# One plain chunk instead of two at the start of each feed-forward block, and a new order of products and operand sums

## The chip, the cores and the metric

The kernel runs on one core of one Trainium2 chip. The metric is the device time of one execution in microseconds (us). Smaller is better.

## The reference

The trunk has two layers. A layer is half a feed-forward block, a token mixer (HGRN2 in layer 0, windowed attention in layer 1), and half a feed-forward block again, each behind an RMSNorm; so there are four feed-forward blocks, called f0 to f3 here. The tokens of both requests (512 and 256) share the weights.

```
D_MODEL = 1024; D_FF = 2816; DEPTH = 2
def swiglu_ffn(x, w1, w2):                     # all float32
    gate, up = jnp.split(x @ w1, 2, axis=-1)   # w1: 1024 x 5632
    return (jax.nn.silu(gate) * up) @ w2       # w2: 2816 x 1024
for li in range(DEPTH):
    x = x + 0.5 * swiglu_ffn(rmsnorm(x, norm_g[li, 0]), ffn_w1[li, 0], ffn_w2[li, 0])
    x = x + mixer(rmsnorm(x, norm_g[li, 1]))   # hgrn2_mixer, then window_gqa_mixer
    x = x + 0.5 * swiglu_ffn(rmsnorm(x, norm_g[li, 2]), ffn_w1[li, 1], ffn_w2[li, 1])
return rmsnorm(x, final_norm_g)
```

## The kernel before

**Products.** A float32 product is three matmuls: each operand is split into a high part (a cast on ScalarE) and a low part (a subtraction on VectorE), and TensorE multiplies high by high, high by low, low by high into one bank of PSUM (`mm3`, L288 to L290, and `product`, L527). `split` (L293 and L294) does it for operands, L229 and L230 for weights, L186 and L189 for the weights of plain chunks.

**Seven products.** The feed-forward blocks use a Strassen-Winograd form. The 768 tokens are two halves of 384 columns, the model width is two halves of 512. The turned (transposed) token blocks are b00, b10, b01, b11, and four sums of them are t1 to t4. Product p1 multiplies a weight block with b00, p2 with b10, p3 with b11, p4 with t4, p5 with t1, p6 with t2, p7 with t3. One chunk is 128 hidden columns. A chunk by seven products (`up_pair`) is 7 x 4 x 3 = 84 matmuls of 384 columns; a plain chunk (`up_plain`, two token halves, gate and up column, eight blocks of the width) is 2 x 2 x 8 x 3 = 96. A block has 22 chunks: two plain ones (0 and 1), whose first half needs only b00 and b10, then twenty by seven products. After each group of four chunks the down products follow (`down_quad`, L608).

**Operand sums.** When the second token half has been turned and split (b01, b11), `sums` makes t1 to t4: for each of two column groups `kp` four subtractions (L441, L442, L444, L445) and four splits of 128 x 768 elements. VectorE does them while TensorE works on the plain chunks.

**Weights.** SyncE's queue (SP) loads the raw blocks: two "wr" tiles of 512 KB (gate, up) and one "s" tile of 256 KB (for p7) a chunk. There are four wr buffers and two s buffers. GpSimd (POOL) issues accumulating transfers: s += first block of wr, and in place wr += wr (L153). VectorE adds twice into wr (L243), for p6 and p3. `split` in `quad_steps` makes one "w" tile for each product (L229, L230); there are eight. `plan_ffn` queues the loads, `load_next` issues a load when raw buffers are free, and `ahead` stages the next product's weights whenever TensorE frees a w tile.

**Order.** Each engine works in its own order, which a tile scheduler derives from the program's order, the dependences and a few hints (`issue_after`). So the diff alone does not give the order on an engine. In the rows of this order "waits" names what an instruction waits for: an engine (Activation is ScalarE, Pool is GpSimd), a transfer of SP's queue (DMAHW) or one of GpSimd's (DMASW).

Of the kernel before, what the change touches and what calls it, by code (L numbers as in the profile page):

```python
# [49 lines left out]
class Trunk:  # L50
    def __init__(self, ctx, tc, consts):
# [103 lines left out]
    def load_next(self):  # L155
# [43 lines left out]
    def quad_steps(self, key, raws, srcs, order):  # L199
# [36 lines left out]
        sums = {"p6": (a11, a21), "p3": (a12, a11)}  # L236
        last = [None]

        def step(name):
            if name in sums:  # L240
                into, term = sums[name]
                with self.tc.issue_after(last[0]):
                    nc.vector.tensor_add(into, into, term)  # L243
# [292 lines left out]
    def up_pair(self, tag, j, hold=False):  # L536
        nc = self.nc
        key = (tag, j)
# [1040 lines left out]
```

## Time and profile before

| | |
|---|---|
| time, median of 3 runs | 2731.84 us (2731.38, 2731.84, 2732.61) |
| span of the profiled execution | 2730.5 us, mean granted TensorE clock 0.999 |
| TensorE (PE) busy | 2720.2 us, 100% |
| VectorE (DVE) busy | 2110.3 us, 77% |
| ScalarE (ACT) busy | 1339.0 us, 49% |
| GpSimd (POOL) busy | 204.8 us, 7% |

The span runs from the first to the last instruction of the profiled execution; for that execution no other time is given, and the three times above are those of the timed runs. The span lies 1.3 us below their median. Matmuls are pipelined, so the duration of one row (334 ns) is longer than the step from one to the next.

### The profile page before, as it was taken

Reading aid. Unit: us, or ns where it says so; the run is one execution under the profiler, and the core shown is the slowest. Engines: PE = TensorE matmul, PEld = TensorE weight load, DVE = VectorE, ACT = ScalarE, POOL = GpSimd, SP = SyncE. Lnnn points to the kernel's source line nnn. Section 1 sums busy time; section 2 is a strip of 40 time slices with the busy share of each in tenths; the row PEclk is TensorE's granted clock in tenths of the full one; section 3 lists DMA queues with packets and bytes.
Section 4 is the critical chain, followed back from the end, with each engine's and each line's share of the span. In section 5 each row is a group of like instructions: output and inputs, shape, how many; then the busy total and the mean of one; then the engine's idle time right before and its main releaser. Section 6 shows DMA issues by size and latency. Waiting matters only on the chain.

```text
span 2730.5 us, 44549 instructions
## 1 busy us (share of the span) xinstructions
PE 2720.2 (100%) x17305; PEld 2483.8 (91%) x17305; DVE 2110.3 (77%) x3789; ACT 1339.0 (49%) x2507; POOL 204.8 (7%) x243
## 2 busy tenths in 40 slices
PE   9999999999999999999999999999999999999998
PEld 9999999889888889999999999999987789999998
DVE  8888788567476778778888878887847768787877
ACT  6444444456466554444446444444546754444443
POOL 1110110000000000111110011101000000111000
PEclk9999999999999999999999999999999999999999
DMA  6544554311110524465553355544422123555443
GB/s 183 136 123 117 127 143 120 123 56 48 55 41 25 143 65 120 113 147 129 128 121 102 88 129 139 135 116 112 133 72 78 47 62 87 130 139 135 117 112 108
DMA packets 331411, 293.98 MB, mean 108 GB/s; under 512 B 11752, under 2 KB 258240, under 8 KB 331200
## 3 DMA queue, kind: packets, MB, share of 16 engines
q1 hardware_dynamic: 294352, 212.89, 26.6%
q0 software_dynamic: 32544, 64.76, 13.6%
q10 hardware_dynamic: 4304, 13.49, 1.4%
q8 instruction: 135, 2.21, 0.3%
q14 instruction: 76, 0.62, 0.1%
HBM read 216.91 MB, written 9.44 MB: 83 GB/s over the span
## 4 chain that ended last, share of the span: by engine, by line
PE 97%; DVE 1%; ACT 1%; issue 0%; DMA 0%; DVEq 0%; SPq 0%; ACTq 0%
PE ps L527 42%; PE ps L608 21%; PE ps L288 9%; PE ps L289 9%; PE ps L290 9%; PE ps L856 1%; PE ps L643 1%; PE ps L1451 1%; PE ps L1442 1%; PE ps L1004 1%; PE ps L1390 1%; PE ps L411 1%; PE ps L980 0%; PE ps L969 0%; DVE x L671 0%
## 5 line engine op out<-in xcount | busy, mean ns | idle before, releaser
L527 PE MATMUL ps<-big,w 128*128 128x384 f32 x6720 | 1169.7, 334 | 0.6 <-ACT tA L544 0.6
L527 PEld LDWEIGHTS ps<-big,w 128*128 128x128 f32 x6720 | 1165.9, 188 | 2.8 <-ACT tA L544 1.2
L229 ACT CAST w<-wr 128x512 fp32r<-128x512 f32 (+1 forms) x606 | 424.2, 710 | 721.8 <-DVE wr L243 305.4
L230 DVE TENSOR_TENSOR w<-wr,w 128x512 fp32r<-128x512 f32 (+1 forms) x606 | 480.5, 798 | 225.4 <-ACT w L229 158.5
L608 PE MATMUL ps<-w,big 128*128 128x512 f32 x2520 | 575.4, 389 | 0.0
L608 PEld LDWEIGHTS ps<-w,big 128*128 128x128 f32 x2520 | 472.8, 188 | 97.5 <-DVE x L671 0.3
L671 DVE SCALAR_TENSOR_TENSOR x<-ps,x 128x512 f32<-128x512 f32 x468 | 302.6, 681 | 4.7 <-PE ps L290 4.7
L288 PE MATMUL ps<-w,big 128*128 128x512 f32 x576 | 232.5, 404 | 0.0
L290 PE MATMUL ps<-w,big 128*128 128x512 f32 x576 | 225.5, 391 | 0.0
L289 PE MATMUL ps<-w,big 128*128 128x512 f32 x576 | 225.1, 391 | 0.0
L288 PE MATMUL ps<-big,w 128*128 128x384 f32 (+2 forms) x640 | 217.9, 342 | 0.2
L289 PE MATMUL ps<-big,w 128*128 128x384 f32 (+2 forms) x640 | 215.8, 337 | 0.4 <-DVE big L371 0.2
L290 PE MATMUL ps<-big,w 128*128 128x384 f32 (+2 forms) x640 | 215.1, 336 | 0.0
L293 ACT CAST big<-tA 128x384 fp32r<-128x384 f32 x296 | 147.8, 512 | 117.5 <-DVE tA L572 40.4
L153 POOL DMA_DIRECT2D s<-wr x122 | 106.3, 913 | 1300.1 <-DMA wr<-in_ffn_w_dram 623.6
L189 DVE TENSOR_TENSOR w<-wr,w 128x1024 fp32r<-128x1024 f32 (+1 forms) x88 | 105.9, 1209 | 82.0 <-ACT w L186 73.4
L294 DVE TENSOR_TENSOR big<-tA,big 128x384 fp32r<-128x384 f32 x296 | 159.9, 551 | 8.2 <-ACT big L293 7.8
L153 POOL DMA_DIRECT2D wr<-wr x101 | 87.6, 868 | 1009.3 <-DVE tA L1110 386.0
L186 ACT CAST w<-wr 128x1024 fp32r<-128x1024 f32 (+1 forms) x90 | 93.0, 1035 | 93.4 <-PE ps L289 66.3
L288 PEld LDWEIGHTS ps<-w,big 128*128 128x128 f32 x576 | 108.3, 188 | 25.6 <-issue 4.6
L290 PEld LDWEIGHTS ps<-w,big 128*128 128x128 f32 x576 | 108.1, 188 | 23.5 <-issue 0.4
L289 PEld LDWEIGHTS ps<-big,w 128*128 128x128 f32 x640 | 121.0, 189 | 9.4 <-DVE big L294 1.0
(191 smaller groups left out, 2891.8 us busy)
## 6 DMA issues: line engine op xcount, KB each, us to landing
wr<-in_ffn_w_dram SPq DMA_DIRECT2D x264, 512.0 KB, 3.9
s<-wr POOLq DMA_DIRECT2D x122, 256.0 KB, 5.1
s<-in_ffn_w_dram SPq DMA_DIRECT2D x120, 256.0 KB, 3.3
wr<-wr POOLq DMA_DIRECT2D x80, 256.0 KB, 4.2
wr<-in_hg_w_in_dram SPq DMA_DIRECT2D x40, 512.0 KB, 3.8
wr<-wr POOLq DMA_DIRECT2D x21, 512.0 KB, 6.0
spill<-x ACTq DMA_DIRECT2D x12, 512.0 KB, 2.9
x<-spill ACTq DMA_DIRECT2D x12, 512.0 KB, 3.3
```

The costliest lines, as they stand in the source:

```text
L153: self.nc.gpsimd.dma_start(out, src, accum_op=ALU.add)
L189: eng.tensor_sub(lo, raw[:, ks, :], hi.bitcast(F32))
L229: nc.scalar.copy(h, src)
L230: low = nc.vector.tensor_sub(l, src, h.bitcast(F32)).ins
L288: nc.tensor.matmul(out, a[0], b[0], start=first, stop=False)
L289: nc.tensor.matmul(out, a[0], b[1], start=False, stop=False)
L290: nc.tensor.matmul(out, a[1], b[0], start=False, stop=last)
L293: self.nc.scalar.copy(hi, src)
L294: return self.nc.vector.tensor_sub(lo, src, hi.bitcast(F32)).ins
L527: self.nc.tensor.matmul(ps, a[x], b[y], start=first and k == 0 and i == 0, stop=k == 3 and i == 2, skip_group_check=True,)
L608: nc.tensor.matmul(ps, a[x], w[y], start=name == chain and kp == 0 and q == 0, stop=kp == 1 and q == 2, skip_group_check=True,)
L671: return self.nc.vector.scalar_tensor_tensor(x, ps, c, x, ALU.mult, ALU.add).ins
```

## The change

In each block only chunk 0 stays plain. Chunk 1 becomes a chunk by seven products, and chunks 1 and 2 are opened early (`open_pair`): behind the plain half 0 come p1 and p2 of both, then the plain half 1, then p3, p3, p5, p7, p5, p4, p6, p7 of the two in turn, and p6 and p4 of chunk 2. The weights of their p3 are made ahead of the operand sums: four additions into raw blocks and two splits, behind the last split of b11 (`turned`). The sums are made in the order t1, t3, t4, t2, each for both column groups. Chunk 3 does its products in another order (`THIRD`). `closed` and `open` hold back the staging of further weights until a given product is done.

```diff
--- before.py
+++ after.py
-PLAIN = 2
-GROUPS = (NF - PLAIN) // 4
+GROUPS = (NF - 2) // 4
+OPEN = ("p1", "p2", "p3", "p5", "p7", "p4", "p6")
+OPEN2 = ("p1", "p2", "p3", "p5", "p7", "p6", "p4")
+THIRD = ("p1", "p4", "p2", "p7", "p5", "p6", "p3")
...
+        if how is OPEN:
+            self.loaded.append((2, steps[:2]))
+            self.opened = steps[2:]
+        elif how is OPEN2:
+            a, b = self.opened, steps[2:]
+            self.loaded.append((0, steps[:2]))
+            entries = [(2, [a[0], b[0], a[1], a[2], b[1], a[3], a[4]]), (2, b[2:])]
+            self.closed.append(entries[0])
+            self.loaded += entries
+        elif how is THIRD:
+            self.loaded += [(0, steps[:3]), (2, steps[3:])]
+            self.closed.append(self.loaded[-1])
+        else:
+            self.loaded.append((len(raws), steps))
...
-        sums = {"p6": (a11, a21), "p3": (a12, a11)}
+        sums = {"p6": [(a11, a21)], "p3": [(a12, a11)]}
+        if order in (OPEN, OPEN2):
+            sums = {"p3": sums["p6"] + sums["p3"]}
         last = [None]
 
         def step(name):
-            if name in sums:
-                into, term = sums[name]
-                with self.tc.issue_after(last[0]):
+            for into, term in sums.get(name, ()):
+                low = self.turned if order in (OPEN, OPEN2) else last[0]
+                with self.tc.issue_after(last[0]), self.tc.issue_after(low):
                     nc.vector.tensor_add(into, into, term)
             last[0] = split(name, own[name])
...
+            if self.closed and self.loaded[0] is self.closed[0]:
+                return
             if self.held + self.loaded[0][1][0][0] > WBUFS:
                 return
             self.stage_next()
+
+    def open(self):
+        if self.closed:
+            self.closed.pop(0)
...
+            self.turned = low
...
-        for kp in range(2):
-            tiles = (self.tn[(i // 2, i % 2)][:, kp] for i in range(4))
-            self.mix(*tiles, lambda name, src: self.put(name, kp, src))
+        sub = self.nc.vector.tensor_sub
+        both = lambda f: [f(kp, *tiles[kp]) for kp in range(2)]
+        both(lambda kp, b11, b12, b21, b22: (sub(b22, b12, b22), sub(b12, b11, b12), self.put("t1", kp, b12)))
+        both(lambda kp, b11, b12, b21, b22: self.put("t3", kp, b22))
+        both(lambda kp, b11, b12, b21, b22: (sub(b11, b11, b22), sub(b21, b21, b11), self.put("t4", kp, b21)))
+        both(lambda kp, b11, b12, b21, b22: self.put("t2", kp, b11))
...
-            if i < PLAIN:
+            if i == 0:
                 self.plan((tag, i, 0), gate, (NC, P))
                 self.plan((tag, i, 1), up, (NC, P))
             else:
-                self.plan_quad((tag, i), (gate, up), (NC, P), UP)
+                self.plan_quad((tag, i), (gate, up), (NC, P), {1: OPEN, 2: OPEN2, 3: THIRD}.get(i, UP))
...
             if half:
+                if not c:
+                    self.open()
                 self.done((tag, j, c))
...
+        third = j == 3
...
-        p("p7", c, True, False)
+        p("p4" if third else "p7", c, True, False)
         nc.scalar.copy(w, c)
-        free("p7")
+        free("p4" if third else "p7")
         p("p2", a, False, True)
         nc.scalar.activation(a, a, AF.Silu)
         free("p2")
+        if third:
+            p("p7", c, False, True)
+            nc.vector.tensor_sub(w, c, w)
+            free("p7")
         p("p5", d, True, False)
         nc.vector.tensor_sub(w, w, d)
         free("p5")
-        p("p4", c, False, True)
+        if not third:
+            p("p4", c, False, True)
         p("p6", b, True, True)
         nc.vector.tensor_sub(v, v, b)
         nc.vector.tensor_sub(t, c, v)
         nc.vector.tensor_mul(t, t, a)
-        free("p4", "p6")
+        free(*(("p6",) if third else ("p4", "p6")))
...
+    def open_pair(self, tag, j, hold):
+        nc = self.nc
+        banks = {}
...
+        def gate():
+            p("p1", "a", True, False)
+            nc.scalar.copy(v, banks["a"])
+            free("p1")
+            p("p2", "a", False, True)
+            nc.scalar.activation(banks["a"], banks["a"], AF.Silu)
+            free("p2")
...
+        def p3():
+            p("p3", "d", True, False)
+            nc.scalar.copy(w, banks["d"])
+            free("p3")
+
+        def p5():
+            p("p5", "d", False, True)
+            free("p5")
+
+        def p7():
+            p("p7", "c", True, False)
+            nc.vector.tensor_add(w, w, banks["c"])
+            nc.vector.tensor_sub(w, w, banks["d"])
+            free("p7")
+
+        def p4():
+            p("p4", "c", False, True)
+            free("p4")
+
+        def p6():
+            p("p6", "b", True, True)
+            nc.vector.tensor_sub(v, v, banks["b"])
+            free("p6")
+        def results():
+            t = self.tmp(H)
+            nc.vector.tensor_sub(t, banks["c"], v)
+            nc.vector.tensor_mul(t, t, banks["a"])
+            yield t
+            nc.vector.tensor_sub(w, w, v)
+            nc.vector.tensor_add(v, v, banks["d"])
...
+            pairs = {}
             if g == 0:
-                ts = {}
-                for half in range(2):
-                    for j in range(PLAIN):
-                        t = ts[2 * j + half] = self.up_plain(tag, j, half)
-                        name = f"b{j}{half}"
...
-                gather(ts, 0)
+                first = [self.up_plain(tag, 0, 0)]
+                low = put("b00", first[0], 0)
...
+                gate, p3, p5, p7, p4, p6, results = zip(*(self.open_pair(tag, j, j == 2) for j in (1, 2)))
+                gate[0]()
+                gate[1]()
+                for j in (1, 2):
+                    self.take((tag, j, "p3"))
                 self.run_later(len(self.deferred))
+                first.append(self.up_plain(tag, 0, 1))
+                for step in (p3[0], p3[1], p5[0], p7[0], p5[1], p4[0], p6[0], p7[1]):
+                    step()
+
+                def second():
+                    p6[1]()
+                    self.open()
+                    p4[1]()
+                    yield from results[1]()
+
+                pairs[1], pairs[2] = results[0](), second()
+                pairs[0] = first
             for kp in range(2):
                 ts = []
                 for j in range(2):
-                    for half, t in enumerate(self.up_pair(tag, 4 * g + 2 * kp + j, j == 0)):
+                    n = 4 * g + 2 * kp + j
+                    for half, t in enumerate(pairs.get(n) or self.up_pair(tag, n, j == 0)):
                         ts.append(t)
                         name = f"b{j}{half}"
-                        if name != "b01":
+                        if name != "b01" and (n or half):
                             put(name, t, kp)
                 gather(ts, kp)
             self.down_quad(tag, g, hid)
```

The order on the engines shows it at three places. The first is VectorE in f0 at the last split of b11. Before, the sums follow at once (rows L441 to L445; L453 is an addition that `sums` does first).

```order
L294 TENSOR_TENSOR big_74_399<-big_70_382,big_74_399 128x2x384 [waits Activation_49]
L294 TENSOR_TENSOR big_75_402<-big_70_382,big_75_402 128x2x384 [waits Activation_49]
L453 TENSOR_TENSOR big_39_220<-big_36_204 128x768
L453 TENSOR_TENSOR big_39_220<-big_37_211 128x768
L441 TENSOR_TENSOR big_70_382<-big_63_343,big_70_382 128x768 [waits DVE_49] x2
L442 TENSOR_TENSOR big_63_343<-big_34_198,big_63_343 128x768 [waits DVE_49] x2
L444 TENSOR_TENSOR big_34_198<-big_34_198,big_70_382 128x768 [waits DVE_49]
L294 TENSOR_TENSOR big_77_422<-big_63_343,big_77_422 128x2x384 [waits Activation_49]
L445 TENSOR_TENSOR big_39_220<-big_39_220,big_34_198 128x768 [waits DVE_49]
```

After, big_76 and big_77 are b11's split; the four additions into the raw blocks of chunk 1 (wr_23, wr_24) and chunk 2 (wr_43, wr_44) and the two splits of p3's weights (w_79, w_80) come next, and then the sums.

```order
L318 TENSOR_TENSOR big_77_408<-big_72_388,big_77_408 128x2x384 [waits Activation_49]
L261 TENSOR_TENSOR wr_23_157<-wr_23_157,wr_24_159 128x512 [waits DMAHW5_49,DMASW2_49,DMASW1_49]
L261 TENSOR_TENSOR wr_43_231<-wr_43_231,wr_44_233 128x512 [waits DMASW6_49,DMASW5_49,DMAHW0_49,DVE_49,Pool_49]
L261 TENSOR_TENSOR wr_23_157<-wr_23_157 128x512 [waits DVE_49]
L261 TENSOR_TENSOR wr_43_231<-wr_43_231 128x512 [waits DVE_49]
L478 TENSOR_TENSOR big_40_224<-big_38_215 128x768
L246 TENSOR_TENSOR w_79_440<-wr_23_157,w_79_440 128x512 [waits PE_49,Activation_49]
L246 TENSOR_TENSOR w_80_445<-wr_43_231,w_80_445 128x512 [waits PE_49,Activation_49]
L483 TENSOR_TENSOR big_72_388<-big_65_348,big_72_388 128x768 x2
L483 TENSOR_TENSOR big_65_348<-big_35_202,big_65_348 128x768 [waits DVE_49] x2
L485 TENSOR_TENSOR big_35_202<-big_35_202,big_72_388 128x768 [waits DVE_49]
L318 TENSOR_TENSOR big_81_452<-big_65_348,big_81_452 128x2x384 [waits Activation_49]
```

The p3 weights moved ahead of every sum. The second addition waits for two transfers of GpSimd's queue (DMASW5, DMASW6). Behind these rows stand three splits, two sums and then the split of w_90, the weights of chunk 1's p5.

The second place is TensorE in f0, where the product p5 of chunk 1 starts. Before, the plain chunks run until the first seven-product chunk starts with p1 (ps_106), p7 (ps_108) behind it.

```order
L527 MATMUL ps_106_621<-big_32_186,w_88_495 128x384 [waits Activation_49]
L527 MATMUL ps_106_621<-big_32_186,w_88_495 128x384
L527 MATMUL ps_106_621<-big_32_186,w_88_495 128x384 [waits DVE_49]
L527 MATMUL ps_106_621<-big_32_186,w_88_495 128x384 x3
L527 MATMUL ps_106_621<-big_33_193,w_88_495 128x384 x6
L527 MATMUL ps_108_623<-big_79_430,w_89_498 128x384 [waits PE_49,Activation_49]
L527 MATMUL ps_108_623<-big_79_430,w_89_498 128x384
L527 MATMUL ps_108_623<-big_79_430,w_89_498 128x384 [waits DVE_49]
L527 MATMUL ps_108_623<-big_79_430,w_89_498 128x384 x3
```

After, ps_103 ends p3 of chunk 2, ps_106 is p7 of chunk 1 (weights w_91), ps_101 with w_90 is p5 of chunk 1 and ps_103 with w_92 p5 of chunk 2.

```order
L558 MATMUL ps_103_578<-big_76_405,w_80_445 128x384 x3
L558 MATMUL ps_103_578<-big_77_408,w_80_445 128x384 x6
L558 MATMUL ps_106_610<-big_83_460,w_91_510 128x384 [waits PE_49,Activation_49]
L558 MATMUL ps_101_561<-big_81_452,w_90_507 128x384 [waits Activation_49]
L558 MATMUL ps_101_561<-big_81_452,w_90_507 128x384 [waits DVE_49]
L558 MATMUL ps_106_610<-big_83_460,w_91_510 128x384 [waits DVE_49]
L558 MATMUL ps_103_578<-big_81_452,w_92_513 128x384 [waits Activation_49]
L558 MATMUL ps_103_578<-big_81_452,w_92_513 128x384
L558 MATMUL ps_101_561<-big_81_452,w_90_507 128x384 [waits DVE_49]
L558 MATMUL ps_101_561<-big_81_452,w_90_507 128x384 x3
L558 MATMUL ps_101_561<-big_82_457,w_90_507 128x384 x6
L558 MATMUL ps_106_610<-big_83_460,w_91_510 128x384 [waits DVE_49]
```

Six matmuls of three products stand ahead of the rest of p5 of chunk 1, which waits for VectorE.

The third place is VectorE in f1, around the last products of the two opened chunks. Before, chunk 2 (ps_1266 is its p5) has the engine to itself with splits of its own raw blocks (wr_1202, wr_1203).

```order
L294 TENSOR_TENSOR big_1261_10385<-tA_1257_10369,big_1261_10385 128x384 [waits Activation_49]
L294 TENSOR_TENSOR big_1262_10388<-tA_1230_10146,big_1262_10388 128x384 [waits Activation_49]
L230 TENSOR_TENSOR w_1272_10443<-wr_1203_10002,w_1272_10443 128x512 [waits DMASW0_49,DMAHW3_49,PE_49,Activation_49]
L556 TENSOR_TENSOR tA_1268_10396<-tA_1268_10396,ps_1266_10394 128x384 [waits PE_49]
L230 TENSOR_TENSOR w_1273_10459<-wr_1203_10002,w_1273_10459 128x512 [waits Activation_49]
L243 TENSOR_TENSOR wr_1202_10000<-wr_1202_10000,wr_1203_10002 128x512
L230 TENSOR_TENSOR w_1274_10490<-wr_1202_10000,w_1274_10490 128x512 [waits Activation_49]
```

After, ps_1272 holds p7 of chunk 2, and L652 reads it before p4 of chunk 2 adds into the same bank; w_1267, w_1269, w_1270 and w_1281 are the weights of chunk 3's p1, p4, p2 and p7, from wr_1258, wr_1259 and s3_1260.

```order
L246 TENSOR_TENSOR w_1267_10395<-wr_1258_10335,w_1267_10395 128x512 [waits DMAHW4_49,Activation_49]
L246 TENSOR_TENSOR w_1269_10413<-wr_1259_10337,w_1269_10413 128x512 [waits DMAHW5_49,Activation_49]
L246 TENSOR_TENSOR w_1270_10428<-wr_1258_10335,w_1270_10428 128x512 [waits Activation_49]
L246 TENSOR_TENSOR w_1281_10527<-s3_1260_10339,w_1281_10527 128x512 [waits DMAHW3_49,DMASW3_49,Activation_49]
L662 TENSOR_TENSOR tA_1235_10170<-tA_1235_10170,ps_1271_10443 128x384 [waits PE_49]
L667 TENSOR_TENSOR tA_1273_10472<-ps_1268_10398,tA_1235_10170 128x384 [waits DVE_49]
L670 TENSOR_TENSOR tA_1236_10171<-tA_1236_10171,tA_1235_10170 128x384
L668 TENSOR_TENSOR tA_1273_10472<-tA_1273_10472,ps_1239_10174 128x384 [waits DVE_49]
L652 TENSOR_TENSOR tA_1238_10173<-tA_1238_10173,ps_1272_10457 128x384 [waits PE_49]
```

The split of p7's weights of chunk 3 (w_1281), which waits for a transfer of SP (DMAHW3) and one of GpSimd (DMASW3), now stands ahead of L652 of chunk 2. On TensorE the matmul that adds p4 of chunk 2 into ps_1272 waits for that L652.

```order
L558 MATMUL ps_1272_10457<-big_1246_10251,w_1261_10343 128x384 x6
L558 MATMUL ps_1280_10501<-big_1249_10264,w_1264_10363 128x384 x6
L558 MATMUL ps_1280_10501<-big_1250_10267,w_1264_10363 128x384 x6
L558 MATMUL ps_1272_10457<-big_1247_10256,w_1266_10380 128x384 [waits DVE_49,Activation_49]
L558 MATMUL ps_1272_10457<-big_1247_10256,w_1266_10380 128x384 x5
L558 MATMUL ps_1272_10457<-big_1248_10261,w_1266_10380 128x384 x6
L558 MATMUL ps_1292_10563<-big_1201_9995,w_1267_10395 128x384 [waits Activation_49]
```

More of the change, by code (lines that the diff above doesn't have):

```diff
@@ L170, in load_next @@
             steps = self.quad_steps(key, raws, srcs, how)
-        self.loaded.append((len(raws), steps))
+        if how is OPEN:
[12 more added lines that the diff above has]
+            self.loaded.append((len(raws), steps))
     def wtile(self):
@@ L454, in sums @@
         self.whole = []
-        for kp in range(2):
-            tiles = (self.tn[(i // 2, i % 2)][:, kp] for i in range(4))
-            self.mix(*tiles, lambda name, src: self.put(name, kp, src))
+        tiles = [[self.tn[(i // 2, i % 2)][:, kp] for i in range(4)] for kp in range(2)]
+        sub = self.nc.vector.tensor_sub
[4 more added lines that the diff above has]
+        both(lambda kp, b11, b12, b21, b22: self.put("t2", kp, b11))
     xn = [None] * NBLK
     normed = mixed = first = halved = None
-    normal = None
+    normal = opened = turned = None
     plains = 0
@@ L509, in up_plain @@
                     self.first = None
-                if half == 0 and k in (((), (2, 6)), ((3, 7), (3, 7)))[j][c]:
+                if half == 0 and c and k in (2, 6):
                     self.run_later()
             if half:
+                if not c:
+                    self.open()
                 self.done((tag, j, c))
@@ L579, in up_pair, with p, free, finish @@
         yield w
+    def open_pair(self, tag, j, hold):
+        nc = self.nc
+        banks = {}
+        v, w = (self.tmp(H) for _ in range(2))
+        def p(name, bank, first, last):
+            if first:
+                banks[bank] = self.ps(H)
+            self.product((tag, j), name, FACTOR[name], banks[bank], first, last)
+        def free(name):
+            self.done((tag, j, name))
+        def gate():
+            p("p1", "a", True, False)
+            nc.scalar.copy(v, banks["a"])
+            free("p1")
+            self.run_later(len(self.deferred) > 1)
+            p("p2", "a", False, True)
+            nc.scalar.activation(banks["a"], banks["a"], AF.Silu)
+            free("p2")
+            self.run_later(len(self.deferred) > 1)
+        def p3():
[24 more added lines that the diff above has]
+            nc.vector.tensor_add(v, v, banks["d"])
+            def finish(after=None):
+                with self.tc.issue_after(after) if after else nullcontext():
+                    self.last_act = nc.scalar.activation(v, v, AF.Silu).ins
+                self.last_dve = nc.vector.tensor_mul(w, v, w).ins
+            if hold:
+                self.tail = finish
+            else:
+                finish()
+            yield w
+        return gate, p3, p5, p7, p4, p6, results
     def down_quad(self, tag, g, hid):
@@ L683, in gather @@
                 self.mix(ts[0], ts[1], ts[2], ts[3], lambda name, src: put(name, src, kp))
+            pairs = {}
             if g == 0:
-                ts = {}
-                for half in range(2):
-                    for j in range(PLAIN):
-                        t = ts[2 * j + half] = self.up_plain(tag, j, half)
-                        name = f"b{j}{half}"
-                        if name != "b01":
-                            low = put(name, t, 0)
-                        if name == "b00" and self.whole:
-                            with self.tc.issue_after(low):
-                                for parts in self.whole[:2]:
-                                    self.nc.vector.tensor_add(*parts)
-                            del self.whole[:2]
@@ L698, in ffn @@
-                gather(ts, 0)
-                self.run_later(len(self.deferred))
+                first = [self.up_plain(tag, 0, 0)]
+                low = put("b00", first[0], 0)
+                if self.whole:
+                    with self.tc.issue_after(low):
+                        for parts in self.whole[:2]:
+                            self.nc.vector.tensor_add(*parts)
+                    del self.whole[:2]
+                gate, p3, p5, p7, p4, p6, results = zip(*(self.open_pair(tag, j, j == 2) for j in (1, 2)))
@@ L700, in ffn @@
+                pairs[1], pairs[2] = results[0](), second()
+                pairs[0] = first
             for kp in range(2):
-                if g == 0 and kp == 0:
-                    continue
                 ts = []
                 for j in range(2):
-                    for half, t in enumerate(self.up_pair(tag, 4 * g + 2 * kp + j, j == 0)):
+                    n = 4 * g + 2 * kp + j
+                    for half, t in enumerate(pairs.get(n) or self.up_pair(tag, n, j == 0)):
                         ts.append(t)
```

2 lines of the change are left out of this document (1 added, 1 removed).

## The prediction

> **What bounds the kernel now.** I read the clock first, then the page, then what TensorE waits for.
>
> ```profile
> core 0: 2730.5 us, clock 0.999
> PE 2720.2 (100%) x17305; PEld 2483.8 (91%) x17305; DVE 2110.3 (77%) x3789; ACT 1339.0 (49%) x2507; POOL 204.8 (7%) x243
> PE 97%; DVE 1%; ACT 1%; issue 0%; DMA 0%; DVEq 0%; SPq 0%; ACTq 0%
> ```
>
> ```profile
> PE ps L104 <- DVE eps L101: 1.1, 1, 1.1
> PE ps L527 <- ACT tA L544: 0.6, 1, 0.6
> ```
>
> TensorE is busy all the time, and 97% of the chain that ended last is its own. The largest wait inside the run is one of 0.6 us. So the time is the number of matmuls by their step, and whatever the change takes off TensorE counts in full unless a new wait eats it.
>
> The step comes from a stretch of 168 matmuls of 384 columns in f1, its start and the start of what follows (columns: start, length, line, count):
>
> ```profile
> 1030.91 29.28 PE L527 MATMUL ps<-big,w 128*128 128x384 f32 x168
> 1060.03 2.24 PE L608 MATMUL ps<-w,big 128*128 128x512 f32 x9
> ```
>
> (1060.03 - 1030.91) / 168 = 0.1733 us. Plain matmuls (L288 to L290) start as closely: the four plain columns that start at 1014.27 below end at 1030.91, 96 matmuls in 16.64 us, 0.1733 each.
>
> **The gain.** A plain chunk is 96 matmuls, a chunk by seven products 84. Four blocks lose 12 each: 48 x 0.1733 = 8.32 us. Nothing else leaves TensorE.
>
> **What it costs.** The first token half must now cover less. VectorE does the work that the change moves: four additions and two splits of 512 columns per block ahead of the sums. Rows of VectorE in f1 that stand without a pause give the price and the start of the sums:
>
> ```profile
> 1007.09 1.83 DVE L294 TENSOR_TENSOR big<-big,big 128x768 fp32r<-128x768 f32 x2 [1.60 <-ACT big L293]
> 1008.83 0.95 DVE L441 TENSOR_TENSOR big<-big,big 128x768 f32<-128x768 f32 x1
> ...
> 1015.65 2.68 DVE L294 TENSOR_TENSOR big<-big,big 128x768 fp32r<-128x768 f32 x3
> 1018.26 0.95 DVE L442 TENSOR_TENSOR big<-big,big 128x768 f32<-128x768 f32 x1
> ...
> 1026.01 0.55 DVE L294 TENSOR_TENSOR big<-tA,big 128x384 fp32r<-128x384 f32 x1
> 1026.47 1.89 DVE L230 TENSOR_TENSOR w<-wr,w 128x512 fp32r<-128x512 f32 x3
> 1028.28 0.68 DVE L243 TENSOR_TENSOR wr<-wr,wr 128x512 f32<-128x512 f32 x1
> ```
>
> ```profile
> 1014.27 0.33 PE L288 MATMUL ps<-big,w 128*128 128x384 f32 x1
> ```
>
> A 768 column operation costs (1018.26 - 1015.65) / 3 = 0.87 us, one of 512 columns (1028.28 - 1026.47) / 3 = 0.60, one of 384 columns 0.46. The second plain half starts at 1014.27.
>
> **f1, f2, f3: the sums.** TensorE up to plain half 1 is as long as before (half 0 of 48 matmuls, then 48 of p1 and p2 in place of 48 plain ones), so half 1 still starts at 1014.27. It ends 8.32 us later, at 1022.59; the two p3 take 24 x 0.1733 = 4.16, and p5 of chunk 1 starts at 1026.75. From b11's last split to the split of p5's weights the new order gives VectorE 4 additions, 3 splits of 512 columns, 11 operations of 768 and 2 of 384: 7 x 0.60 + 11 x 0.87 + 2 x 0.46 = 14.7 us, from 1008.83 to 1023.5. That is 3.2 us early; TensorE's 12.5 us of half 1 and p3 are the cover. Without it the 3.7 us of moved additions and splits would show. I cost it at nothing in these three blocks. In f2 VectorE starts the sums at the same distance from TensorE's second stretch of 48 matmuls (in f1 1008.83 - 1005.93 = 2.90 us):
>
> ```profile
> 1005.93 0.35 PE L288 MATMUL ps<-big,w 128*128 128x384 f32 x1
> ...
> 1495.88 0.34 PE L288 MATMUL ps<-big,w 128*128 128x384 f32 x1
> ```
>
> ```profile
> 1498.78 0.95 DVE L441 TENSOR_TENSOR big<-big,big 128x768 f32<-128x768 f32 x1
> ```
>
> I take f3 as alike.
>
> **f0: the sums.** Here the operands come late.
>
> ```profile
> 30.42 1.82 DVE L294 TENSOR_TENSOR big<-big,big 128x768 fp32r<-128x768 f32 x2
> 32.16 1.82 DVE L453 TENSOR_TENSOR big<-big 128x768 f32<-128x768 f32 x2
> ...
> 47.52 2.69 DVE L294 TENSOR_TENSOR big<-big,big 128x768 fp32r<-128x768 f32 x3
> 50.13 0.55 DVE L294 TENSOR_TENSOR big<-tA,big 128x384 fp32r<-128x384 f32 x1
> ```
>
> ```profile
> 48.35 5.88 PE L527 MATMUL ps<-big,w 128*128 128x384 f32 x33
> ```
>
> Before, t3 is ready at 50.13 and p7 wants it at 48.35 + 12 x 0.1733 = 50.43: already only 0.3 us to spare. After, TensorE has 168 matmuls ahead of p5 instead of 192 ahead of the first p1, and reaches p5 at 48.35 - 24 x 0.1733 = 44.19. VectorE ends b11's split and one L453 at 33.03, the first addition at 33.63; from the second addition (call its start X) to p5's split it has 6 operations of 512 and 12 of 768 columns, 14.1 us. With X = 33.63 p5's weights are ready at 47.7. TensorE can do six early matmuls (1.04 us) and then stands still from 45.2: 2.5 us at least. Behind it VectorE stays the later one: up to p7's weights it needs 2 x 0.87 + 0.60 = 2.3 us more, where TensorE has ten matmuls, 1.7 us, and similar differences of 0.3 and 0.5 us follow at p6 and p4, with some given back by what TensorE does meanwhile. So 0.9 to 1.4 us more.
>
> X also waits for GpSimd's sixth and seventh transfer. Before, GpSimd issued like this:
>
> ```profile
> 22.61 0.86 POOL L153 DMA_DIRECT2D x<-x  x1 [0.45 <-issue]
> 25.38 0.89 POOL L153 DMA_DIRECT2D wr<-wr  x1 [1.90 <-issue]
> 28.56 0.87 POOL L153 DMA_DIRECT2D s<-wr  x1 [2.30 <-issue]
> 30.80 0.88 POOL L153 DMA_DIRECT2D s<-wr  x1 [0.85 <-issue]
> 34.05 0.86 POOL L153 DMA_DIRECT2D wr<-wr  x1 [2.38 <-DVE big L453]
> ```
>
> and over 15 to 40 us its transfers and SP's took (last number: median us to landing)
>
> ```profile
> wr<-in_ffn_w_dram SPq DMA_DIRECT2D x4, 512.0 KB, 7.6
> s<-wr POOLq DMA_DIRECT2D x2, 256.0 KB, 5.5
> ```
>
> The steps of 2.2 to 3.2 us between issues have idle time put down to "issue", as if only three were under way at once. The sixth at 30.80 and a seventh 2.7 later, at 33.5, landing 5.5 us on, would give X = 39.0, and a first wait of 39.0 + 14.1 - 45.2 = 7.9. But chunk 3's raws (1.25 MB) are no longer loaded at that time, and GpSimd's transfers share only with each other. I take X = 34.4, near the low end, for that reason: 3.3 + 0.9 = 4.2 us for f0, with ends 3.4 and 9.3.
>
> **f1 to f3: chunk 3's weights.** Before, chunk 3's raws lay ready long ahead. After, its two wr blocks go into buffers that only the splits for p4 and p6 of chunk 1 free. By the rows above VectorE ends these at about 1030.0 and 1030.6. Then SP loads, GpSimd adds into s, ScalarE casts, VectorE splits. In before's trace from 1026 to 1048 us, and over the whole run, this costs:
>
> ```profile
> wr<-in_ffn_w_dram SPq DMA_DIRECT2D x4, 512.0 KB, 3.5
> s<-wr POOLq DMA_DIRECT2D x2, 256.0 KB, 4.5
> ```
>
> ```profile
> wr<-in_ffn_w_dram SPq DMA_DIRECT2D x264, 512.0 KB, 3.9
> s<-wr POOLq DMA_DIRECT2D x122, 256.0 KB, 5.1
> ```
>
> ```profile
> 467.01 0.62 ACT L229 CAST w<-wr 128x512 fp32r<-128x512 f32 x1 [4.12 <-DVE wr L243]
> ```
>
> 1030.05 + 3.8 (load) + 0.7 (GpSimd's start) + 4.2 (add) + 0.6 (cast) + 0.6 (split) = 1039.95. Five rows of 0.46 us follow on VectorE, the last of them L652, which reads p7's bank of chunk 2: 1042.0 or slightly later. TensorE, without other waits, has done p7 of chunk 2 at 1039.2 and p6 at 1041.3, and then wants to add p4 into that bank: a wait of 0.7 us (0.2 to 1.4 with the add at 3.3 to 5.1). In f2 the split of chunk 3's p5, behind GpSimd's second add, also stands ahead of L652: 1.5 us (0.9 to 2.7). In f0 this split stands behind L652, and I cost it at nothing. SP's queue stands at the first of these loads until 1030, and behind it are only the second one and the loads for the group's down weights; GpSimd has the adds for the same weights behind its two. TensorE wants them after chunk 3's 84 matmuls, 14.6 us, which I take to hide them; without that cover a wait would show at the first down product.
>
> The added rows beside this are cheap: 28 on ScalarE, 56 on VectorE over the run, where ScalarE is half idle, and eight more transfers by GpSimd, which is 7% busy.
>
> **Sum.** - 8.32 + 4.2 (f0) + 0.7 + 1.5 + 0.7 = - 1.2 us. From the median of 2731.84: 2730.6. (The span of the profiled execution would go from 2730.5 to 2729.3.) A difference under 0.2%, 5.5 us, can't be told from none here, so this is "no change". Its own range, with all ends, is 2728 to 2736.
>
> **A rule to weigh.** The one wait of the trace (0.6 us, at 473) is followed by matmuls at the usual step:
>
> ```profile
> 473.18 4.11 PE L527 MATMUL ps<-big,w 128*128 128x384 f32 x22 [0.60 <-ACT tA L544]
> ```
>
> 22 matmuls in 4.11 us, and the mean clock is 0.999. A wait of 3.3 us is not in the trace. If a long wait made TensorE's clock fall to half for about as long as the wait, the next 3.4 us would do half the work: 1.7 us more, 2732.3.
> The Trainium skill ("TensorE: Matmul & The Clock Gate", section "What's actually happening") says that after one idle window of about 3.4 us the clock gate passes 4 of 8 pulses, and goes back after a busy window; the window is free-running. No run here shows that yet; by it f0's wait of 2.5 to 3.3 us is just too short, and a longer one is not.
>
> **Rivals.**
> - *The cover suffices.* In f1 to f3 the loads and adds take their short values (3.5 and 3.3) and nothing waits; in f0 b11's split ends earlier, since the VectorE pauses ahead of it (1.6 us in the f1 row above is of the same kind) shrink. f0 then waits 1.4 us and the time is 2731.84 - 8.32 + 1.4 = 2724.9. Against it: 14.1 us of VectorE rows from 33.6 on, with no pause in them. It decides if all waits together stay under 2.8 us.
> - *Chunk 3's raws come late* (the other side). The loads and adds of f1 to f3 take what they took in f0's start: 5.5 instead of 3.8 to load, 5.5 instead of 4.2 to add, 3.0 us more a block, 9.0 in all, 2739.6. For it: the load is two blocks and two adds at once, and staggered. Against it: the rows of 1026 to 1048. It decides (slower by 0.2%) from 2.2 us more a block.
> - *The clock falls* behind f0's wait, 2732.3 as above; still no change.
>
> That the change doesn't take the matmuls away is no rival: the order has 12 fewer in each block.
>
> **Chances.** No change as summed 0.53, the clock rival 0.06, the cover 0.28, late raws 0.13. So faster 0.28, same 0.59, slower 0.13. The range reaches to the cover's value and to most of the late raws: 2724.9 to 2737.
>
> **What would show it.** Right: 48 fewer matmuls of 384 columns at an unchanged 0.173 us; in the list of TensorE's waits one at L558 (p5) near 45 us of some 3 us, ended by VectorE; one of 0.5 to 1.5 us near 1041 in f1 and its like in f2 and f3, ended by L652; none at the start of p3. Wrong: no wait near 45 us, or VectorE's sums of f0 starting well before 33 us (the cover), or waits above 3 us at p4 of chunk 2 or at chunk 3's p7 (late raws), or a step above 0.2 us behind f0's wait (the clock).

## The result, and the profile after

| | before | changed |
|---|---|---|
| median | 2731.89 us (2731.38 to 2732.61) | 2751.98 us (2750.1 to 2752.26) |
| ratio | 1 | 1.0072, 95% interval 1.0057 to 1.0086 |
| profiled execution | span 2730.5 us | 2750.1 us, span 2748.3 us |

The change costs 20 us: 2752 us, where 2730.6 was forecast. The times are medians, and one of the ten executions of the kernel before with six buffers (experiment 4), a slow one of 3878 us at a clock of 0.65, is left out. The page and the clock of the changed kernel (`product` is L558 here, `mm3` L312 to L314, `down_quad` L713, `split` L317 and L318, weights L245 and L246):

```profile
core 0: 2748.3 us, clock 0.997
PE 2721.3 (99%) x17257; PEld 2480.7 (90%) x17257; DVE 2134.9 (78%) x3849; ACT 1348.6 (49%) x2535; POOL 211.3 (8%) x251
PE 92%; DVE 3%; DMA 2%; ACT 1%; issue 1%; POOL 0%; DVEq 0%; SPq 0%; POOLq 0%; ACTq 0%
```

TensorE has the 48 matmuls fewer that were promised, and still it is busy 1 us longer: some matmuls run slower. And the chain, 97% TensorE before, now leaves it for 8%. What TensorE waits for, the five longest (us in total, times, longest):

```profile
PE ps L558 <- ACT big L317: 6.7, 2, 3.9
PE ps L558 <- DVE tA L652: 2.6, 1, 2.6
PE ps L558 <- ACT tA L576: 2.6, 1, 2.6
PE ps L558 <- DVE w L246: 2.1, 1, 2.1
PE ps L558 <- DVE tA L592: 1.9, 1, 1.9
```

The timeline of TensorE places them: f0 (two), f1, f2 (two), f3. The first row is a stretch without a wait, for comparison.

```profile
1012.51 8.51 PE L558 MATMUL ps<-big,w 128*128 128x384 f32 x48
...
48.54 4.79 PE L558 MATMUL ps<-big,w 128*128 128x384 f32 x17 [2.07 <-DVE w L246]
72.75 5.49 PE L558 MATMUL ps<-big,w 128*128 128x384 f32 x21 [2.60 <-ACT tA L576]
1052.05 10.13 PE L558 MATMUL ps<-big,w 128*128 128x384 f32 x48 [3.88 <-ACT big L317]
1544.98 15.23 PE L558 MATMUL ps<-big,w 128*128 128x384 f32 x84 [2.61 <-DVE tA L652]
1562.35 2.36 PE L558 MATMUL ps<-big,w 128*128 128x384 f32 x12 [1.90 <-DVE tA L592]
2300.42 3.81 PE L558 MATMUL ps<-big,w 128*128 128x384 f32 x14 [2.82 <-ACT big L317]
```

The profile puts the waits of f1 and f3 down to a cast on ScalarE (L317), but in f1 that cast ended at 1051.98 and L652, which the order names too, at 1051.90; the cast itself waited for L668, the row ahead of L652. Both stand behind the same split, so the cause below is one.

48 matmuls take 8.51 us, but 10.13 us behind f1's wait: 1.6 us more. The starts of single matmuls there lie 0.32 us apart for 10 matmuls, then 0.173 again. Counted from start to start, beyond the usual step and with the slow matmuls, the places cost: f0's p5 5.1 us (waits of 0.7, 0.3 and 2.2, then 1.9 slow), f0's chunk 3 4.4 (2.8 and 1.7), f1 5.7 (4.0 and 1.65), f2 2.9 with no half-speed matmuls and 2.1 + 0.3 at the end of chunk 3, f3 4.6 (3.0 and 1.6). Sum 25.1, less 8.3 saved: 16.8 of the 17.8 us between the two spans. (The profiled execution is the shortest of the four. The other three are 1.6 to 2.2 us longer, at a clock of 0.995 to 0.996; one more stretch of slow matmuls would fit, but they have no trace.)

Why f1 waits is seen on four queues between 1032 and 1052 us (SP, GpSimd, ScalarE, VectorE):

```profile
1036.60 3.19 SPq L167 DMA_DIRECT2D wr<-in_ffn_w_dram  x4
1041.21 0.89 POOL L156 DMA_DIRECT2D s<-wr  x1 [50.41 <-DMA wr<-in_ffn_w_dram]
1048.11 0.62 ACT L245 CAST w<-s 128x512 fp32r<-128x512 f32 x1 [4.57 <-DMA s<-wr]
1048.76 0.69 DVE L246 TENSOR_TENSOR w<-s,w 128x512 fp32r<-128x512 f32 x1 [4.42 <-ACT w L245]
1051.35 0.55 DVE L652 TENSOR_TENSOR tA<-tA,ps 128x384 f32<-128x384 f32 x1
```

SP issues four loads within 3.2 us, as the four buffers come free: two are chunk 3's, two are already the group's down weights. GpSimd's add into s then takes 6.7 us:

```profile
wr<-in_ffn_w_dram SPq DMA_DIRECT2D x4, 512.0 KB, 4.8
s<-in_ffn_w_dram SPq DMA_DIRECT2D x1, 256.0 KB, 7.0
s<-wr POOLq DMA_DIRECT2D x1, 256.0 KB, 6.7
```

(1034 to 1048 us; in f2 and f3 the adds took 5.6 and 5.5, in f0 6.5.) The cast stands 4.57 us at the head of ScalarE's queue, the split 4.42 us at the head of VectorE's, and L652, which needs none of it, is the fifth row behind.

### The profile page after: what moved, and what is told of

Same layout as the page of the kernel before. It is cut to its first block, busy times and chain, and to the rows that moved or that the text cites. A ratio compares the mean times of both kernels' runs of the same rounds, so it can differ in the third digit from the quotient of the medians.

```text
span 2748.3 us, 44577 instructions
## 1 busy us (share of the span) xinstructions
PE 2721.3 (99%) x17257; PEld 2480.7 (90%) x17257; DVE 2134.9 (78%) x3849; ACT 1348.6 (49%) x2535; POOL 211.3 (8%) x251
## 4 chain that ended last, share of the span: by engine, by line
PE 92%; DVE 3%; DMA 2%; ACT 1%; issue 1%; POOL 0%; DVEq 0%; SPq 0%; POOLq 0%; ACTq 0%
PE ps L558 41%; PE ps L713 21%; PE ps L312 8%; PE ps L313 7%; PE ps L314 7%; PE ps L972 1%; PE ps L748 1%; PE ps L1567 1%; PE ps L1558 1%; PE ps L1120 1%; PE ps L1506 1%; DMA wr<-in_ffn_w_dram 1%; DVE big L318 1%; PE ps L435 1%; DMA s<-wr 1%
## 5 line engine op out<-in xcount | busy, mean ns | idle before, releaser
L558 PE MATMUL ps<-big,w 128*128 128x384 f32 x7056 | 1238.9, 336 | 16.7 <-ACT big L317 6.7
L558 PEld LDWEIGHTS ps<-big,w 128*128 128x128 f32 x7056 | 1230.0, 189 | 22.7 <-ACT big L317 7.3
L245 ACT CAST w<-wr 128x512 fp32r<-128x512 f32 (+1 forms) x630 | 437.5, 707 | 707.9 <-DVE wr L261 292.2
L246 DVE TENSOR_TENSOR w<-wr,w 128x512 fp32r<-128x512 f32 (+1 forms) x630 | 495.1, 793 | 210.6 <-ACT w L245 146.0
L713 PE MATMUL ps<-w,big 128*128 128x512 f32 x2520 | 576.0, 389 | 0.0
L713 PEld LDWEIGHTS ps<-w,big 128*128 128x128 f32 x2520 | 472.6, 188 | 97.6 <-DVE x L776 0.3
L312 PE MATMUL ps<-w,big 128*128 128x512 f32 x576 | 232.5, 404 | 0.0
L314 PE MATMUL ps<-w,big 128*128 128x512 f32 x576 | 225.5, 391 | 0.0
L317 ACT CAST big<-tA 128x384 fp32r<-128x384 f32 x296 | 147.9, 513 | 126.9 <-DVE tA L599 37.7
L312 PE MATMUL ps<-big,w 128*128 128x256 f32 (+2 forms) x512 | 174.6, 343 | 0.1
L313 PE MATMUL ps<-big,w 128*128 128x256 f32 (+2 forms) x512 | 172.9, 338 | 0.5 <-DVE big L395 0.2
L314 PE MATMUL ps<-big,w 128*128 128x256 f32 (+2 forms) x512 | 172.1, 336 | 0.0
L318 DVE TENSOR_TENSOR big<-tA,big 128x384 fp32r<-128x384 f32 x296 | 159.8, 551 | 10.3 <-ACT big L317 10.2
L205 DVE TENSOR_TENSOR w<-wr,w 128x1024 fp32r<-128x1024 f32 (+1 forms) x80 | 96.2, 1208 | 81.5 <-ACT w L202 73.1
L312 PEld LDWEIGHTS ps<-w,big 128*128 128x128 f32 x576 | 108.3, 188 | 25.7 <-issue 4.6
L202 ACT CAST w<-wr 128x1024 fp32r<-128x1024 f32 (+1 forms) x82 | 84.5, 1034 | 92.4 <-PE ps L313 66.3
L314 PEld LDWEIGHTS ps<-w,big 128*128 128x128 f32 x576 | 108.1, 188 | 23.5 <-issue 0.4
L313 PEld LDWEIGHTS ps<-w,big 128*128 128x128 f32 x576 | 108.5, 188 | 19.7
```

Of the source, the lines that this page charges most:

```text
L205: eng.tensor_sub(lo, raw[:, ks, :], hi.bitcast(F32))
L245: nc.scalar.copy(h, src)
L246: low = nc.vector.tensor_sub(l, src, h.bitcast(F32)).ins
L312: nc.tensor.matmul(out, a[0], b[0], start=first, stop=False)
L313: nc.tensor.matmul(out, a[0], b[1], start=False, stop=False)
L314: nc.tensor.matmul(out, a[1], b[0], start=False, stop=last)
```

## The experiments

Three theories: **A**, chunk 3's accumulating transfers are late, and in-order queues pass the lateness on; **R**, the deeper cause is that the two opened chunks hold all four wr buffers; **P**, it is only the place of chunk 3's late splits in the order. Against them **B**: VectorE has too much work behind the sums; and **C**: SP's loads are late, not the adds. And **H**: TensorE's clock falls behind a long wait.

**1. The add into s on GpSimd itself.**

```diff
-            self.into(t, a11[:, i * 512 : (i + 1) * 512])
+            src = a11[:, i * 512 : (i + 1) * 512]
+            if order is THIRD:
+                nc.gpsimd.tensor_add(t, t, src)
+            else:
+                self.into(t, src)
```

> Changed kernel, but the addition into chunk 3's s tile is done by GpSimd itself (one tensor_add, about 1.3 us by GpSimd's split row at the start) and not by an accumulating transfer (5.5 to 6.7 us here); the order on the other engines stays. Theory A, the late accumulating transfers: the waits of 4.04 us (f1) and 2.99 us (f3) ahead of p4 of chunk 2 go, with the half-speed matmuls behind them, 5.7 + 4.6 us; f2 keeps its wait, because the split behind the second transfer stands ahead of L652 there, and f0 keeps its wait behind the same second transfer on ScalarE: about 2741.7. Theory B, VectorE has too much work: the waits stay, 2750 to 2752. Theory C, the loads by SP are late and not the adds: under 1 us less a block, above 2748.

2743.91 us (ratio to before 1.0042, 95% interval 1.0029 to 1.0055). Theory A's figure was missed by 2 us, C's by 4, B's by 6. The add takes 1.28 us, the split starts at 1044.36 and L652 comes in time:

```profile
1040.80 1.28 POOL L233 TENSOR_TENSOR s<-s,wr 128x512 f32<-128x512 f32 x1 [50.00 <-DMA wr<-in_ffn_w_dram]
1044.36 0.69 DVE L250 TENSOR_TENSOR w<-s,w 128x512 fp32r<-128x512 f32 x1
1071.94 8.23 PE L717 MATMUL ps<-w,big 128*128 128x512 f32 x35 [1.58 <-DVE x L780]
```

f1 and f3 lose their waits at L652; f0 and f2 keep theirs, as forecast, but shorter (1.8 and 1.7 us). The third row is what took the place in f1: a wait in the down products, one of four over the run, 4.0 us in all, which theory A had not counted.

**2. Both adds of chunk 3 on GpSimd itself** (also `nc.gpsimd.tensor_add(a21, a21, a22)` for chunk 3).

> As the run before, and the second addition of chunk 3 (wr += wr) is done by GpSimd itself too. Theory A: the waits at chunks 2 and 3 go in all four blocks, 4.4 + 5.7 + 2.9 + 4.6 = 17.6 us less than the changed kernel: about 2734; what is left over the time before is f0's wait at p5 with its half-speed matmuls (5.1) and f2's late down weights (2.1). Theory B: 2750 to 2752. Theory C: above 2747.

2745.35 us (1.0049, 1.0036 to 1.0061): 11 us above theory A, 1.7 below C. The waits at L652 are gone in all blocks, but the end of chunk 3 now waits for 2.0 to 2.7 us in f1, f2 and f3. In f1 ScalarE, VectorE:

```profile
1061.80 1.05 ACT L251 CAST w<-wr 128x1024 fp32r<-128x1024 f32 x1 [3.83 <-DMA wr<-in_ffn_w_dram]
1062.88 1.23 DVE L252 TENSOR_TENSOR w<-wr,w 128x1024 fp32r<-128x1024 f32 x1 [1.98 <-ACT w L251]
1064.49 0.55 DVE L598 TENSOR_TENSOR tA<-tA,ps 128x384 f32<-128x384 f32 x1
```

The same form one step on, and here it is a load by SP that is late: a split of down weights whose raw block arrives late stands ahead of L598, which reads the bank of chunk 3's p5 before p3 adds into it. The lateness was passed on, not removed.

**3. Two plain chunks in f0 only.** f0 plans and runs chunks 0 and 1 plain and the rest in `UP` order; f1 to f3 stay changed.

> Changed kernel, but f0 has two plain chunks and the old course of products as before; f1 to f3 as changed. f0 then loses its wait at p5 of chunk 1 (5.1 us with the half-speed matmuls) and the one at chunk 3's p2 (4.4), and pays 12 matmuls, 2.1 us: 7.4 us less than the changed kernel, about 2744.4. If f0's waits were only passed on from the blocks' common course (VectorE too full everywhere), the later blocks would not care either, so the same; if the clock fall is no real cost, 3.2 + 2.8 - 2.1 = 3.9 less, about 2748.

2744.05 us (1.0046, 1.0032 to 1.0059), as forecast with the slow matmuls counted, and 4 us below the figure without them. f0's chunks 2 and 3 run again without a wait, 168 matmuls in 29.28 us:

```profile
48.06 29.28 PE L560 MATMUL ps<-big,w 128*128 128x384 f32 x168
```

f0's share of the loss is its own; f1 to f3 keep theirs.

**4. Six wr buffers.** `RAWBUFS = 6`; the room comes from `SLOTS = 20` and 7 tA tiles. With it a control with the same room and four wr buffers, one with six buffers in the kernel before, and one with two plain chunks in f0.

> Changed kernel with six wr buffers instead of four (room made by 20 instead of 21 operand slots and 7 instead of 8 tA tiles). Theory R, the four wr buffers, which the two opened chunks hold until about 1036 us in f1, make chunk 3's loads late, and behind them the down weights' loads: chunk 3's raws are there 30 us early, the waits at L652 and at the end of chunk 3 go in all blocks (about 20 us), f0's wait at p5 with its half-speed matmuls (5.1 us) stays: 2731.9 - 8.3 + 5.1 = about 2728.7. Theory B (VectorE has too much work behind the sums): 2745 or more, as with the adds on GpSimd.

> Control: changed kernel with 20 operand slots and 7 tA tiles, and four wr buffers as they were. If the smaller room costs nothing: 2752 as the changed kernel, waits at the same places. If it costs something, the difference to 2752 is to be added to what the run with six wr buffers gains.

> Six wr buffers (20 slots, 7 tA), two plain chunks in f0 and the changed course in f1 to f3. Theory R: no wait over 0.7 us is left in the four blocks and 36 matmuls are saved: 2731.9 - 6.2 = 2725.7, faster than both kernels. Theory B: waits of 2 to 4 us in f1 to f3, above 2735.

> Control: kernel before with six wr buffers, 20 slots and 7 tA. TensorE has no waits to lose there: 2731 to 2733. If more raw buffers help or the smaller room costs something by itself, it is seen here.

| | us | ratio to before (95%) |
|---|---|---|
| changed, six buffers | 2739.42 | 1.0025 (1.0015 to 1.0035) |
| changed, same room, four | 2757.76 | 1.0093 (1.0079 to 1.0107) |
| changed, six, two plain in f0 | 2731.25 | 0.9997 (0.9988 to 1.0006) |
| before, six buffers | 2736.79 | 1.0017 (1.0008 to 1.0026) |

The smaller room is not free: 5.8 us in the changed kernel, and 4.6 us in the kernel before (whose waits don't grow; 40 of its down products start 0.30 to 0.34 us apart instead of 0.227, against one with the full room; why, was not followed). Against its control six buffers gain 18.3 us, and no wait ahead of p4 of chunk 2 or in chunk 3 is left in any block; TensorE's longest waits with six buffers and two plain chunks in f0 (the first lies at the start, the second in the attention):

```profile
PE ps L107 <- DVE eps L104: 1.1, 1, 1.1
PE ps L1525 <- ACT tA L1579: 0.7, 1, 0.7
PE ps L435 <- ACT big L438: 0.4, 1, 0.4
```

Against the kernel before with six buffers that run is 5.5 us faster, where 36 matmuls are worth 6.2. The absolute figures were missed by the cost of the room, and by f0, whose waits at p3 and p5 with six buffers come to 9.5 us with the slow matmuls. Theory R is borne out as one cure; B falls.

**5. The splits later, with four buffers.** The casts of chunk 3's p7 and p5 weights go behind ScalarE's copy of chunk 3's p1:

```diff
-            last[0] = split(name, own[name])
+            late = order is THIRD and name in ("p7", "p5")
+            with self.tc.issue_after(self.copied) if late else nullcontext():
+                last[0] = split(name, own[name])
...
         turned = nc.scalar.copy(v, a).ins
+        if third:
+            self.copied = turned
+            self.open()
...
-                    self.open()
```

`open`, which releases the staging of the weights of chunk 3's last four products, moves to that copy too (before, behind p6 of chunk 2).

> Changed kernel; the casts and splits of chunk 3's p7 and p5 weights are placed behind the copy of chunk 3's own p1 on ScalarE, so that L652 of chunk 2 no longer stands behind them. Rival P, only the place in the order is wrong: the raws are in time for p7 of chunk 3, the waits at chunk 2 and chunk 3 go in all blocks (about 17 us) and nothing takes their place: about 2735. Theory R, the four wr buffers make everything behind them late: the waits at L652 go, and 1.5 to 2.5 us a block come back later, at chunk 3's p7, p5 or at the down products: 2740 to 2745.

2735.0 us (1.0009, 1.0000 to 1.0018). The rival P was right, though I had not expected it after the two runs on GpSimd; that it came out to the microsecond is partly luck, since f2's wait for down weights (2.1 us) went as well, and nine small waits of 0.3 to 0.9 us, 4.3 us in all, came in. VectorE in f1:

```profile
1043.75 0.54 DVE L657 TENSOR_TENSOR tA<-tA,ps 128x384 f32<-128x384 f32 x1
1051.89 0.69 DVE L246 TENSOR_TENSOR w<-s,w 128x512 fp32r<-128x512 f32 x1
```

L657 (L652 before) now stands ahead of the split, which is done at 1052.6 and disturbs nobody. GpSimd's add is no faster than in the changed kernel (7.1 us in f1, 5.8 and 5.5 in f2 and f3). The longest waits of TensorE that are left in the four blocks:

```profile
PE ps L560 <- DVE w L246: 2.4, 2, 2.1
PE ps L560 <- ACT tA L578: 1.7, 3, 0.8
PE ps L718 <- DVE x L781: 0.9, 4, 0.4
```

The 2.1 us in the first is f0's p5. So late raws alone did not cost the 17 us: what waited for them stood ahead of others. Why the down weights are in time here and not in experiment 2 was not followed further; their place in the order moved too.

**6. Both cures of the order and f0.** Experiment 5 with two plain chunks in f0.

> The version that the runs point to: two plain chunks and the old course in f0, the changed course in f1 to f3 with the splits of chunk 3's p7 and p5 behind ScalarE's copy of its p1. 36 matmuls fewer, 6.2 us; the small waits that the run with later splits kept in f1 to f3 (about 2.9 us) stay: about 2728.6, faster than both kernels by 0.1%. If f0's waits were needed as slack for the later blocks, or new waits come up: 2731 or more.

2731.73 us, 0.9996 (0.9987 to 1.0005): not told apart from before, and 3 us above the forecast; new waits came up. f0's p5 no longer waits; but the down products, in f0 too, now wait for VectorE 2.1 us in five places, and p2 of the chunk behind them for ScalarE 1.3 us in f1 and f2 together; by starts the products of 512 columns, these waits included, take 3.3 us more over the run than in the kernel before. No version here beats the kernel before.

**7. Waits of set length**, in the kernel before. Extra copies `nc.scalar.copy(v, a)` ahead of p2 in 16 chunks, the second time with TensorE's products held in their written order.

> Kernel before, with 8 to 14 more ScalarE copies of p1's bank (0.41 us each) ahead of p2 in four chunks of each block, 179 copies in all: TensorE gets 16 waits of about 1.7 to 4.2 us, 48 us in all. Theory H, a long wait makes TensorE's clock fall to half for some time: behind the waits above about 2.8 us (some of those from 2.2 us on) 10 matmuls stand at 0.32 us instead of 0.173, 1.6 us each, behind the short ones not: 2731.9 + 48 + about 16 = 2796. Without it: the step stays 0.173 behind every wait, and the time is about 2780.

> Kernel before, with 6 to 13 more ScalarE copies of p1's bank (0.51 us from one to the next) ahead of p2 in four chunks of each block, and TensorE's products held in their written order in these chunks: 16 waits of about 1 to 4.6 us, some 45 us in all. Theory H: behind waits up to 1.8 us the step stays at 0.173 us, behind those over about 3.2 us 8 to 10 matmuls stand at 0.32 us (1.2 to 1.5 us more), between the two it happens in some and not in others: 2732 + 45 + 12 = about 2789. If the fall of the clock needs an idle time of 3.4 us and more, none of the waits below 3.4 is followed by slow matmuls.

The first run missed: the order let TensorE take other products meanwhile, the 16 waits were 0.3 us each, and the time 2741.35. In the second the waits were 2.8 to 6.4 us by starts, 76 us in all and longer than planned, and the time 2838.84. Each was one execution. Two rows of the second:

```profile
157.57 10.67 PE L528 MATMUL ps<-big,w 128*128 128x384 f32 x60 [3.37 <-ACT tA L554]
1779.58 12.24 PE L528 MATMUL ps<-big,w 128*128 128x384 f32 x60 [3.70 <-ACT tA L554]
```

60 matmuls take 10.67 us behind the one and 12.24 behind the other. By the gap between starts beyond the usual step, over all runs (one among attention's small matmuls, and the waits in quick succession in f0 with six buffers, left out):

| wait | followed by matmuls at 0.32 us | not |
|---|---|---|
| 0.76 to 1.83 us | 0 | 14 |
| 2.05 to 3.53 us | 13 | 9 |
| 3.86 to 6.43 us | 15 | 0 |

(Five of the 22 in the middle are f0's p5, 3.6 us behind a shorter wait; without them it is 9 to 8.) Those at 0.32 us begin 0.3 to 1.5 us behind the wait, 7 to 17 in number, and cost 1.0 to 2.5 us. H holds.

What decides in the middle row is in the clock that the traces record, which I had overlooked. In these runs the stretches at 0.50 last 3.41 us or a multiple of it (but for the one at the very end) and begin on a grid of 3.41 us that goes on unbroken through the execution: in the changed kernel at 48.86, 72.75, 1052.38 and 2301.65 us, 7, 287 and 366 steps apart. So a view can be cut along that grid (the changed kernel in f1, then the two rows above; each line has the stretch, its length, the busy time of PE, PEld, VectorE, ScalarE and GpSimd, the clock, the share of DMA and GB/s):

```profile
1048.97:1052.38 3.41, 0.34 (x2) 0.36 (x3) 3.38 (x8) 1.13 (x2) 0.00 (x0) 1.00 0.87 193
1052.38:1055.79 3.41, 3.41 (x13) 3.41 (x12) 3.41 (x7) 1.03 (x2) 0.00 (x0) 0.50 0.00 0
152.38:155.79 3.41, 1.82 (x11) 1.50 (x9) 1.33 (x2) 3.00 (x7) 0.24 (x1) 1.00 1.04 228
155.79:159.20 3.41, 1.63 (x9) 1.63 (x10) 0.56 (x1) 1.85 (x3) 0.00 (x0) 1.00 0.21 37
1777.13:1780.54 3.41, 0.96 (x5) 0.96 (x6) 0.56 (x1) 2.76 (x6) 0.00 (x0) 1.00 0.18 31
1780.54:1783.95 3.41, 3.41 (x13) 3.41 (x12) 0.90 (x2) 0.47 (x1) 0.00 (x0) 0.50 0.00 0
```

The wait of 3.53 us was cut in two by the grid (1.75 and 1.78 us by starts) and cost nothing; the one of 3.86 left 2.45 us in one stretch. So it is over all traces (the first 20 and the last 60 us of each left out): of the stretches at full clock, all 29 in which TensorE stood still for 1.91 us or more by starts were followed by half clock, and none with 1.83 us or less was. This is read from the traces afterwards; no run was made to test it.

## Why the prediction was wrong, point by point

- *The gain.* Right: 48 matmuls at 0.173 us.
- *f1 to f3, the sums.* Right: TensorE doesn't wait at p5 there.
- *f0, the sums.* Right in place and cause: the second addition starts at 34.36 us (34.4 taken), VectorE's split of p5's weights ends at 48.48 (48.5 by the sum), and TensorE's waits come to 3.2 us. The 0.9 us reckoned for waits behind p5 did not come; 1.9 us of slow matmuls, which the sum left out, stood there.
- *f1 to f3, chunk 3's weights.* This step failed by its size. The place (L652 ahead of p4 of chunk 2, behind the split of w_1281) was right, and shifted by the 6.6 us by which f1 runs later, so was the load's issue: 1030.05 + 6.6 = 1036.6. But I took 4.2 us for the add, from a stretch in which transfers come one after another. The loads for the down weights, which the same freed buffers start, I named, but only as something that the matmuls hide; that they run beside the add I left out. The add took 6.7, 5.6 and 5.5 us, the split was ready 2.9 us later than reckoned in f1, L652 ended 2.45 us behind it and not 2.05, and the waits were 4.0, 2.8 and 3.0 us instead of 0.7, 1.5 and 0.7. That the loads lengthen the add is argued, not shown by a run that changes them alone: during f1's 6.7 us SP's queue moved 1.35 MB at DMA engines over 90% busy for most of it, and 0.52 MB during the 4.2 us that I had taken from the kernel before. The rival of late raws gave this course, with a chance of 0.13, and put 3 us more a block on it; the excess was 3.3, 1.3 and 2.3 us of waits (mean 2.3, its deciding point 2.2) and 3.3 us of slow matmuls. So it came true in its course, but its 2739.6 too is 12 us short.
- *f0, chunk 3, costed at nothing.* Wrong, 4.4 us: I looked at VectorE's order, where the split stands behind L652. The cast stands ahead of others on ScalarE all the same. GpSimd's add took 6.5 us here too, ScalarE stood 4.31 us idle until the cast behind it and VectorE 2.96 us until a later cast, and TensorE waited 2.8 us for L576, the copy of chunk 3's p1.
- *The clock.* Weighed for f0 alone, with 0.06 and 1.7 us. It happened there and at three more waits, 6.9 of the 25.1 us. The size per wait was right; the threshold was not: I called a wait of 3.3 us just too short, and one of 2.2 was enough. The Trainium skill ("TensorE: Matmul & The Clock Gate", section "What's actually happening") gives half the clock after an idle window of about 3.4 us. The step of 0.32 us agrees, being 384 columns at its 1.2 GHz; so do the 3.41 us and the grid of the recorded clock, a window of that length that runs freely. That stretches with 1.91 us of standing still are enough does not agree with a fully idle window, and the runs decide.
- *Down weights, costed at nothing.* Wrong in f2, 2.4 us: ScalarE stood 3.79 us at the cast of a down block until its load had landed.
- *The whole.* The span is 19.0 us above the forecast one (2748.3, 2729.3): 10.3 from chunk 3's weights in f1 to f3 (13.2 instead of 2.9, slow matmuls included), 4.4 and 2.4 from the two places costed at nothing, 0.9 from f0's p5; 1.0 us is not placed.
- *Slips in the sums, beside these small.* Five rows of 0.46 us behind 1039.95 end at 1042.25, not 1042.0; adds of 3.3 to 5.1 us move the wait by 0.9 us each way, not by 0.5 and 0.7; and all upper ends together give 2738.3, not 2736.

## What to carry to other kernels

When buffers come free together, price every transfer that they start, not only the one of interest. In engines that work in order, the late item costs by who stands behind it: look for the instruction that waits for a transfer on each in-order queue (ScalarE as well as VectorE), and move it behind what doesn't need it, before looking for memory or faster transfers. And a wait of TensorE can be 1.0 to 2.5 us dearer than it looks: here from 2.1 us on sometimes, from 3.9 us on always.

## What the runs showed that I had not expected

While GpSimd adds from SBUF, a VectorE operation on two SBUF inputs nearly doubles (GpSimd, then VectorE, both adds on GpSimd):

```profile
1040.31 1.29 POOL L233 TENSOR_TENSOR s<-s,wr 128x512 f32<-128x512 f32 x1 [49.90 <-DMA wr<-in_ffn_w_dram]
1040.89 1.25 DVE L252 TENSOR_TENSOR w<-wr,w 128x512 fp32r<-128x512 f32 x1 [1.07 <-ACT w L251]
1044.39 0.68 DVE L252 TENSOR_TENSOR w<-s,w 128x512 fp32r<-128x512 f32 x1
```

1.25 us beside GpSimd's add, 0.68 alone; the twelve such rows of the two runs on GpSimd took 1.25 to 1.65. The Trainium skill ("SBUF — State Buffer", section "SBUF: two separate sides") has the two engines share a pair of ports, which is locked for a whole instruction, a VectorE operation with two SBUF inputs included; these rows agree.
